# A gated recurrence with both heads of a pair on the partition halves, its scores by quarters of the array, and two pieces of other work moved

## The chip, the cores and the metric

The kernel runs on one core of a Trainium2 chip. The metric is the device time of one execution in microseconds (us), the median of several runs. TensorE (PE in the profile) multiplies matrices, VectorE (DVE), ScalarE (ACT) and GpSimd (POOL) do the rest, SyncE (SP) starts most transfers.

## What is computed

Two blocks follow each other on 1024 tokens of width 1024. The first has two layers; each projects tokens and 256 context tokens, mixes them by three mixers, and sends the result through 16 experts of which each takes its best tokens. The mixer that is changed is a gated linear recurrence with 6 heads of 64 keys and 64 values, run forward and backward and added:

```python
def step(s, xs):                       # one chunk of 64 tokens
    qc, kc, gc, vc = xs
    a = jnp.cumsum(gc, axis=2)
    diff = a[:, :, :, None, :] - a[:, :, None, :, :]
    decay = jnp.exp(jnp.where(causal[:, :, None], diff, -jnp.inf))
    scores = jnp.sum(qc[:, :, :, None, :] * kc[:, :, None, :, :] * decay, axis=-1)
    o = jnp.einsum('bhts,bhsv->bhtv', scores, vc) + jnp.einsum('bhtk,bhkv->bhtv', qc * jnp.exp(a), s)
    a_last = a[:, :, -1:, :]
    s_new = jnp.exp(a_last[:, :, 0, :, None]) * s + jnp.einsum('bhsk,bhsv->bhkv', kc * jnp.exp(a_last - a), vc)
    return s_new, o
```

The layer's modulation (shifts, scales and gates) is a product of the condition with `w_mod`. The second block projects into a gated branch, a delta-rule recurrence (16 heads) and 2048 gate columns, and merges them.

## The kernel before

A product of float32 operands is made of three matmuls on a high and a low part of each (`mm3`, lines 168 to 170): high by high, low by high, and high by low. Weights come from HBM as raw tiles and are split into `whi` (ACT, L151) and `wlo` (VectorE or GpSimd, L154). Such projections run in blocks of 24 matmuls, 8 slices of the contraction by 3, of 512 or 256 columns. After each block `tick` advances the generators in `bg`: that is how the recurrence of one pair of heads is laid among the projection blocks of the next columns. In the recurrence's stages `step` is 2, so each block advances it by two yields. The engines work their own instructions in the order written and wait for one another by semaphores.

`hgrn_pair` runs two generators `hgrn_head` alternately. A head has `hQP` and `hKS` on 128 partitions: the forward direction's 64 keys above, the backward one's below. Chunks of 64 tokens are solved by doubling: at level j (0 to 5) the scores of neighbouring blocks of 2^j tokens are made from queries and keys decayed up to the blocks' border. To have both directions in one matmul of 128 partitions, ACT writes masked queries `hZQ` (L532, L533): a block that is a query block forward is zero in the backward half, and the other way round. L515 multiplies 10 or 8 chunks into one PSUM tile, L522 copies what belongs to the level into `hA` (L520 for the diagonal). Then the level's decays follow: two on `hQP` and one on `hKS` by VectorE, the other on `hKS` by GpSimd (L551), each on 64 partitions, and the product of neighbouring totals `hF` (L558). After the levels the keys are transposed (L577), multiplied with the values (L593), the states are run through in 18 steps (L599), copied into the order of the tokens (`hST`, L601 to L603), and the output is made (L617) and copied out.

The stages in question are six, three pairs in each of two layers: the first two beside a projection of gates (one short and two long blocks in turn), the third beside a token projection in short blocks only.

`prologue` makes the modulation: per round of 2048 columns 8 steps, each of a 1 MB load and four matmuls (L196), then the transposes of the result (L210). Round 0 of layer 1 lies in layer 0's output projection, whose last part is the router and the choice of tokens (`tkv`). Round 1 lies at the end of layer 0's experts (4 steps, into tiles of the expert weights) and at the start of layer 1 (4 steps). In the second block `make_hT` transposes the tokens (L282), and the 2048 gate columns are the last projection beside `rw_scan`.

Of the kernel before, what the change touches and what calls it, by code (L numbers as in the profile page):

```python
# [8 lines left out]
F32 = mybir.dt.float32  # L9
# [10 lines left out]
P = 128  # L20
D = 1024
KT = 8
# [20 lines left out]
class Kern:  # L43
# [273 lines left out]
    def gemm_feat(self, w, c0, n, hi, lo, blocks, evac):  # L317

        for c in range(c0, c0 + n, 256):
            m = min(256, c0 + n - c)  # L320
            us = [self.unit(w[512 * h:512 * (h + 1), c:c + m]) for h in range(2)]
            for f in range(0, m, P):
                for (t0, tn) in blocks(c + f):
# [6 lines left out]
                    self.tick()  # L330


class Mixers(Kern):

    def inproj_setup(self):
# [19 lines left out]
        self.fwd = self.const.tile([P, 2], F32, name="fwd")  # L355
        for h in range(2):
            nc.vector.memset(self.fwd[64 * h:64 * h + 64, h:h + 1], 1.0)
            nc.vector.memset(self.fwd[64 * h:64 * h + 64, 1 - h:2 - h], 0.0)
# [104 lines left out]
    def hgrn_pair(self, l, pr, need, pool):  # L463
        nc = self.nc
        T = NT if need else NLAT
        o = pool.tile([P, NT], F32, name="hgo", tag="hgo", bufs=1)

        heads = [self.hgrn_head(l, 2 * pr + j, T, need, o, pool) for j in range(2)]
        for _ in range(3):
            next(heads[0])  # L470
            yield
        while heads:
            for g in list(heads):
                if next(g, self) is self:
                    heads.remove(g)
                else:
                    yield

        y = pool.tile([P, 10, P], F32, name="hgy", tag="hKT", bufs=1).rearrange("p a b -> p (a b)")
# [14 lines left out]

    def hgrn_head(self, l, h, T, need, oT, pool):
        nc = self.nc
        nch = T // 64
        t = lambda nm, n, b: pool.tile([P, n], F32, name=nm, tag=nm, bufs=b)
        QP, KS, F = t("hQP", NT, 2), t("hKS", NT, 2), t("hF", NT, 2)
        r0 = 64 * (h % 2)  # L500
        for d in range(2):
            nc.sync.dma_start(out=QP[64 * d:64 * d + 64, :T], in_=self.d_q[h // 2][r0:r0 + 64, :T])
        nc.sync.dma_start(out=KS, in_=self.d_k[h])
        nc.sync.dma_start(out=F, in_=self.d_f[h])

        V = pool.tile([P, 10, 64], F32, name="hV", tag="hV", bufs=2)
        nc.sync.dma_start(out=V, in_=self.d_vi[:, 384 + h * 64:384 + (h + 1) * 64].rearrange("(i p) c -> p i c", p=P))
        A = pool.tile([P, 10, 64], F32, name="hA", tag="hA", bufs=2)
        npb = nch // 4

        def scores(zq, seg, j):
            ps = self.pt()
            for c in range(2 * npb):
                cc = seg * 2 * npb + c
                nc.tensor.matmul(ps[64 * (c % 2):64 * (c % 2) + 64, c // 2 * 64:c // 2 * 64 + 64], lhsT=KS[:, cc * 64:(cc + 1) * 64],  # L515
                                 rhs=zq[:, c * 64:(c + 1) * 64], start=True, stop=True)
            src = ps[:, :npb * 64].rearrange("p (n t) -> p n t", t=64)
            dst = A[:, seg * npb:(seg + 1) * npb, :]
            if j < 0:
                nc.scalar.copy(dst, src)  # L520
            else:
                nc.vector.copy_predicated(dst, self.smask[:, j, :].unsqueeze(1).to_broadcast([P, npb, 64]), src)  # L522
# [1575 lines left out]
```

## Time and profile before

| | |
|---|---|
| median of 3 runs | 4155.19 us (4153.61 to 4156.73) |
| the profiled execution | 4153.86 us; its span in the trace 4151.9 us |
| TensorE matmul, weight load | busy 3786.7 us (91%), 3056.1 us (74%) |
| VectorE, ScalarE, GpSimd | 2375.6 (57%), 1750.6 (42%), 1220.0 us (29%) |
| granted TensorE clock | 0.959 of full speed, mean |

Busy times overlap, since the engines work side by side. A matmul of float32 operands that doesn't transpose stands in the trace as two rows, so that counts of score rows are twice those of the code. TensorE's matmul rows overlap each other: their rate is read from start to start, not from the length of a row.

### The profile page before, as it was taken

To read this page: it belongs to the slowest core of one execution; us is meant where nothing else is said; L and a number is where in the kernel's file an instruction comes from. 1 tells how busy PE (TensorE), PEld (TensorE's weight loads), DVE (VectorE), ACT (ScalarE), POOL (GpSimd) and SP (SyncE) were. 2 spreads that over 40 slices of the span, in tenths; PEclk is the share of its full clock that TensorE was granted. 3 is DMA by queue.
4 is the path that set the end of the run, shared out by engine and by line. 5 is a ranking of instruction groups with operands and counts; after the bars stand their busy time and mean duration, and the time that the engine had idled before them with its cause. 6 is when DMAs were issued, how large, how long until landed. Compare 5 with 4: busy or idle time off the path is not lost.

```text
span 4151.9 us, 72321 instructions
## 1 busy us (share of the span) xinstructions
PE 3786.7 (91%) x29022; PEld 3056.1 (74%) x29022; DVE 2375.6 (57%) x3761; ACT 1750.6 (42%) x2935; POOL 1220.0 (29%) x1012
## 2 busy tenths in 40 slices
PE   7998999896999989899889599898989999999998
PEld 5877887764677678778777387676768888887777
DVE  3067745657677632774675799756766353332633
ACT  4145543622555432554362376554564212222522
POOL 2134233422233222432442222104551033211630
PEclk9999999998999999999999799999999999999999
DMA  7733322255799874332223799734544544454732
GB/s 244 233 122 105 86 75 82 71 203 176 271 300 307 277 238 146 117 103 76 80 77 129 255 364 370 234 97 125 152 142 136 153 134 130 143 149 138 248 125 91
DMA packets 543791, 695.78 MB, mean 168 GB/s; under 512 B 162400, under 2 KB 350176, under 8 KB 536800
## 3 DMA queue, kind: packets, MB, share of 16 engines
q1 hardware_dynamic: 531360, 653.40, 48.6%
q0 software_dynamic: 12096, 37.75, 3.7%
q8 instruction: 229, 3.75, 0.4%
q14 instruction: 106, 0.87, 0.1%
HBM read 530.61 MB, written 160.43 MB: 166 GB/s over the span
## 4 chain that ended last, share of the span: by engine, by line
PE 38%; DMA 4%; DVE 4%; POOL 3%; issue 2%; ACT 1%; SPq 0%; DVEq 0%; POOLq 0%; ACTq 0%
PE pg L168 10%; PE pg L170 10%; PE pg L169 10%; POOL Xi L1765 1%; PE pt L1932 1%; POOL Xt L1762 1%; PE pt L1836 1%; DMA raw<-in_w_exp_down_dram 1%; PE pg L667 1%; DVE wlo L154 1%; PE pt L840 1%; PE p L804 1%; DMA no<-ro 1%; ACT whi L151 0%; PE pt L771 0%
## 5 line engine op out<-in xcount | busy, mean ns | idle before, releaser
L154 DVE TENSOR_TENSOR wlo<-raw,whi 128x2048 fp32r<-128x2048 f32 (+2 forms) x320 | 597.1, 1876 | 446.8 <-ACT whi L151 446.2
L168 PE MATMUL pg<-hi,whi 128*128 128x512 f32 (+1 forms) x1808 | 720.6, 399 | 2.0 <-DVE cy L457 1.1
L151 ACT CAST whi<-raw 128x2048 fp32r<-128x2048 f32 (+2 forms) x354 | 531.3, 1503 | 443.5 <-PE pg L169 153.0
L170 PE MATMUL pg<-hi,wlo 128*128 128x512 f32 (+1 forms) x1808 | 699.3, 387 | 0.0
L169 PE MATMUL pg<-lo,whi 128*128 128x512 f32 (+1 forms) x1808 | 698.0, 386 | 0.0
L168 PEld LDWEIGHTS pg<-hi,whi 128*128 128x128 f32 x1808 | 347.1, 192 | 78.4 <-issue 6.1
L169 PEld LDWEIGHTS pg<-lo,whi 128*128 128x128 f32 x1808 | 347.4, 192 | 70.7 <-issue 6.8
L170 PEld LDWEIGHTS pg<-hi,wlo 128*128 128x128 f32 x1808 | 346.7, 192 | 68.2
L169 PE MATMUL pg<-wlo,hi 128*128 128x256 f32 x1200 | 343.5, 286 | 6.4 <-DVE wlo L154 3.8
L168 PE MATMUL pg<-whi,hi 128*128 128x256 f32 x1200 | 345.8, 288 | 1.5 <-ACT whi L151 1.1
L170 PE MATMUL pg<-whi,lo 128*128 128x256 f32 x1200 | 343.0, 286 | 0.0
L169 PEld LDWEIGHTS pg<-wlo,hi 128*128 128x128 f32 x1200 | 230.8, 192 | 16.1 <-issue 7.5
L168 PEld LDWEIGHTS pg<-whi,hi 128*128 128x128 f32 x1200 | 230.4, 192 | 14.6 <-issue 8.6
L170 PEld LDWEIGHTS pg<-whi,lo 128*128 128x128 f32 x1200 | 230.8, 192 | 4.1 <-issue 2.8
L154 POOL TENSOR_TENSOR wlo<-raw,whi 128x1024 fp32r<-128x1024 f32 (+1 forms) x34 | 98.3, 2896 | 409.2 <-ACT whi L151 387.9
L168 PE MATMUL pg<-whi,xh 128*128 128x512 f32 x512 | 209.4, 409 | 0.0
L169 PE MATMUL pg<-wlo,xh 128*128 128x512 f32 x512 | 204.9, 400 | 2.2 <-DVE wlo L154 2.1
L170 PE MATMUL pg<-whi,xl 128*128 128x512 f32 x512 | 204.5, 400 | 0.8 <-DVE xl L1066 0.8
L551 POOL TENSOR_TENSOR hKS<-hKS,hF 64x640 f32<-64x640 f32 x72 | 121.2, 1686 | 181.8 <-PE pt L515 132.8
L1130 POOL DMA_INDIRECT x<-eo,iT x32 | 99.3, 3102 | 244.8 <-DVE eo L1122 232.3
L551 DVE TENSOR_TENSOR hQP<-hQP,hF 64x640 f32<-64x640 f32 (+1 forms) x144 | 146.3, 1016 | 10.2 <-ACT hZQ L532 5.3
L1058 POOL DMA_INDIRECT xg<-xn,iT x32 | 61.1, 1911 | 283.9 <-PE pt L1167 266.9
(457 smaller groups left out, 7988.0 us busy)
## 6 DMA issues: line engine op xcount, KB each, us to landing
raw<-in_w_exp_gate_dram SPq DMA_DIRECT2D x64, 1024.0 KB
raw<-in_w_exp_up_dram SPq DMA_DIRECT2D x64, 1024.0 KB
raw<-in_w_exp_down_dram SPq DMA_DIRECT2D x64, 1024.0 KB
raw<-in_k_win_dram SPq DMA_DIRECT2D x124, 512.0 KB
wm<-in_w_mod_dram SPq DMA_DIRECT2D x36, 1024.0 KB
AR<-AR SPq DMA_DIRECT2D x32, 512.0 KB
BK<-BK SPq DMA_DIRECT2D x32, 512.0 KB
mxr<-mix SPq DMA_DIRECT2D x18, 512.0 KB
```

The lines of the kernel that those rows point to most:

```text
L151: nc.scalar.copy(hi, r)
L154: i = eng.tensor_tensor(out=lo, in0=r, in1=f32(hi), op=ALU.subtract)
L168: mm(out, lhsT=lh, rhs=rh, start=start, stop=False)
L169: mm(out, lhsT=lh, rhs=rl, start=False, stop=False)
L170: mm(out, lhsT=ll, rhs=rh, start=False, stop=stop)
L551: eng.tensor_tensor(out=xv, in0=xv, in1=tv[rows, :m, 1 - o].unsqueeze(2).to_broadcast([64, m, s]), op=ALU.mult)
L667: nc.tensor.matmul(po[64 * j:64 * j + 64, :P], lhsT=u["V"][:, u["blk"][x], j * 64:(j + 1) * 64], rhs=u["pT"][:, x, :], start=x == 0, stop= ...
L804: nc.tensor.matmul(ps[:, c0:c0 + n], lhsT=q[:, j, ql], rhs=KK[:, j, k0:k0 + n], start=first, stop=not first, skip_group_check=True)
L840: nc.tensor.transpose(tp[:, x * P:(x + 1) * P], pr[:, (b0 + x) * P:(b0 + x + 1) * P], self.ident)
L1058: nc.gpsimd.indirect_dma_start(out=g, out_offset=None, in_=d_h[:, :], in_offset=bass.IndirectOffsetOnAxis(ap=iT[:, e:e + 1], axis=0))
L1130: nc.gpsimd.indirect_dma_start(out=d_x[:, :], out_offset=bass.IndirectOffsetOnAxis(ap=iT[:, e:e + 1], axis=0), in_=o, in_offset=None, comp ...
L1762: E.tensor_tensor(out=o, in0=Li[:, j, j + 1:].unsqueeze(2).to_broadcast([P, n, m]), in1=X[:, 0, j, :m].unsqueeze(1).to_broadcast([P, n, m] ...
```

## The change

A pair is one generator. Each direction has its tiles `hKS`, `hQP` and `hF`, with the two heads on the partition halves; the columns of the projection are ordered so that the forward gates of a pair stand before its backward ones. A score matmul takes one head (64 partitions), one direction and one chunk, on a quarter of the array; beyond the diagonal it reads only the 32 query columns that count, and writes them to their places in PSUM, a tile for each head. The masked queries and their tiles are gone. The decays are four on 128 partitions, all on VectorE. Each direction has a state tile of its own, read in any order, so that `hST` is gone; the output comes from two PSUM tiles per head (inter-chunk, by direction) and two per parity of chunk, copied by ACT and added by VectorE. Besides, rounds 0 and 1 of layer 1's modulation are both made in layer 0's output projection; and the first 256 gate columns of the second block are projected while its tokens are transposed.

```diff
+            us = [self.split(r) for r in raws or [self.raw(w[512 * h:512 * (h + 1), c:c + m]) for h in range(2)]]
+            order = [(f, b) for f in range(0, m, P) for b in blocks(c + f)]
+            if before:
+                order.sort(key=lambda o: o[1])
+            for i, (f, (t0, tn)) in enumerate(order):
+                    if before:
+                        before(i)
                     acc = self.pg()
...
     def hgrn_pair(self, l, pr, need, pool):
         nc = self.nc
         T = NT if need else NLAT
...
+        nch = T // 64
+        npb = nch // 4
+        dirs, heads = range(2), range(2)
+        half = lambda x: slice(64 * x, 64 * x + 64)
+        t = lambda nm, n, b, tag=None: pool.tile([P, n], F32, name=nm, tag=tag or nm, bufs=b)
+        K = [t("hKS", NT, HB[0]) for d in dirs]
+        Q = [t("hQP", NT, HB[1]) for d in dirs]
+        F = [t("hF", NT, HB[2]) for d in dirs]
...
+        V = pool.tile([P, 10, P], F32, name="hV", tag="hV", bufs=HB[3])
+        A = [pool.tile([P, 10, 64], F32, name="hA", tag="hA", bufs=2) for h in heads]
+        for d in dirs:
+            nc.sync.dma_start(out=Q[d][:, :T], in_=self.d_q[pr][:, :T])
+            nc.sync.dma_start(out=K[d], in_=self.d_k[2 * pr + d])
+            nc.sync.dma_start(out=F[d], in_=self.d_f[2 * pr + d])
...
+        def scores(seg, j):
+
+            ps = [self.pt() for h in heads]
+            for x in range(npb):
+                for d in dirs:
+                    for par in range(2):
+                        cc = 2 * (seg * npb + x) + par
+                        cs = slice(cc * 64, (cc + 1) * 64)
+                        for h in heads:
+                            out, q = ps[h][half(par), x * 64:x * 64 + 64], Q[d][half(h), cs]
+                            if j >= 0:
+                                out, q = (a.rearrange("p (n b s) -> p n b s", b=2, s=1 << j)[:, :, 1 - d, :] for a in (out, q))
+                            nc.tensor.matmul(out, lhsT=K[d][half(h), cs], rhs=q, start=j >= 0 or x + d == 0, stop=j >= 0 or d == 1,
+                                             skip_group_check=True)
+            return ps
+
+        def keep(ps, seg, j):
+            for h in heads:
+                src = ps[h][:, :npb * 64].rearrange("p (n t) -> p n t", t=64)
+                dst = A[h][:, seg * npb:(seg + 1) * npb, :]
+                if j < 0:
+                    nc.scalar.copy(dst, src)
+                else:
+                    nc.vector.copy_predicated(dst, self.smask[:, j, :].unsqueeze(1).to_broadcast([P, npb, 64]), src)
+
+        for seg in range(2):
+            keep(scores(seg, -1), seg, -1)
...
-        y = pool.tile([P, 10, P], F32, name="hgy", tag="hKT", bufs=1).rearrange("p a b -> p (a b)")
+        for d in dirs:
+            nc.vector.tensor_tensor(out=Q[d][:, :T], in0=Q[d][:, :T], in1=F[d][:, :T], op=ALU.mult)
+        Tot = F
+        for j in range(6):
+            s = 1 << j
+            n = NT // (2 * s)
+            tv = [a[:, :2 * n].rearrange("p (n b) -> p n b", b=2) for a in Tot]
+
+            def decay(X, Tn, d, o):
+                m = Tn // (2 * s)
+                xv = X[d][:, :Tn].rearrange("p (n b s) -> p n b s", b=2, s=s)[:, :, o, :]
+                nc.vector.tensor_tensor(out=xv, in0=xv, in1=tv[d][:, :m, 1 - o].unsqueeze(2).to_broadcast([P, m, s]), op=ALU.mult)
+            ps = scores(0, j)
+            yield
+            ps1 = scores(1, j)
+            keep(ps, 0, j)
+            for d in dirs:
+                if j:
+
+                    pv = Tot[d][:, :4 * n].rearrange("p (n b) -> p n b", b=2)
+                    nc.vector.tensor_tensor(out=Tot[d][:, :2 * n], in0=pv[:, :, 0], in1=pv[:, :, 1], op=ALU.mult)
+                decay(Q, T, d, 1 - d)
+                decay(K, NT, d, d)
+            keep(ps1, 1, j)
+            yield
...
+        for d in dirs:
+
+            KT_ = pool.tile([P, 10, P], F32, name="hKT", tag="hKT", bufs=4)
+            for g in range(0, 10, 4):
...
+            yield
...
+            S = pool.tile([P, 20, 64], F32, name="hSP", tag="hKT", bufs=4)
+            pl, pc = self.p2(), [self.pt() for par in range(2)]
+            at = lambda w: pl[:, w % 2 * 512 + w // 2 * 64:][:, :64] if w < 16 else pc[w % 2][:, (w - 16) // 2 * 64:][:, :64]
+            for i in [8, 9] + list(range(8)):
+                for h in heads:
+                    for par in range(2):
+                        c = 2 * i + par
...
+                            nc.tensor.matmul(at(w)[half(h)], lhsT=KT_[half(par), i, half(h)], rhs=V[half(par), i, half(h)], start=True,
+                                             stop=True, skip_group_check=True)
...
+            for w in range(1, 19):
+                c = place(w)
+                nc.vector.scalar_tensor_tensor(out=S[:, w + 1, :], in0=S[:, w, :], scalar=Tot[d][:, c:c + 1], in1=at(w), op0=ALU.mult,
+                                               op1=ALU.add)
+            SP.append(S)
+            yield
+        for c0, cn in [(0, 16)] + ([(16, 4)] if need else []):
...
+            for kind in range(3):
+                for x in range(cn // 2):
+                    for par in range(2):
+                        i = c0 // 2 + x
+                        c = 2 * i + par
+                        xs = slice(x * 64, x * 64 + 64)
+                        for h in heads:
+                            if kind < 2:
+                                nc.tensor.matmul(ps[h][half(par), xs], lhsT=SP[kind][half(h), 19 - c if kind else (c + 4) % 20, :],
+                                                 rhs=Q[kind][half(h), c * 64:(c + 1) * 64], start=kind + x == 0, stop=kind == 1,
+                                                 skip_group_check=True)
+                            else:
+                                nc.tensor.matmul(pa[par][half(h), xs], lhsT=V[half(par), i, half(h)], rhs=A[h][half(par), i, :], start=True,
+                                                 stop=True, skip_group_check=True)
+            for par in range(2):
+                tk = oT[:, c0 * 64:(c0 + cn) * 64].rearrange("p (n b t) -> p n b t", b=2, t=64)[:, :, par, :]
+                v = lambda a: a[:, :cn * 32].rearrange("p (n t) -> p n t", t=64)
+                for h in heads:
+                    nc.scalar.copy(tk[half(h)], v(ps[h][half(par)]))
+                nc.vector.tensor_tensor(out=tk, in0=tk, in1=v(pa[par]), op=ALU.add)
...
-    def hgrn_head(self, l, h, T, need, oT, pool):
...
-        W = T // 2
-        def masked(j):
-            out = []
-            for seg in range(2):
-
-                ZQ = t("hZQ", NT // 2, 4)[:, :W]
-                v = lambda a, o: a.rearrange("p (n b s) -> p n b s", b=2, s=1 << j)[:, :, o, :]
-                q = QP[:, seg * W:(seg + 1) * W]
-                nc.scalar.activation(v(ZQ, 1), v(q, 1), AF.Copy, scale=self.fwd[:, 0:1])
-                nc.scalar.activation(v(ZQ, 0), v(q, 0), AF.Copy, scale=self.fwd[:, 1:2])
-                out.append(ZQ)
-            return out
...
-            decay(QP, T, up, 1, nc.vector)
-            decay(QP, T, dn, 0, nc.vector)
-            if j < 5:
-                ZQ = masked(j + 1)
-            decay(KS, NT, up, 0, nc.vector)
-            decay(KS, NT, dn, 1, nc.gpsimd)
...
-        nc.scalar.copy(ST[0:64], SP[0:64])
-        nc.scalar.copy(ST[64:128, 4:20], SP[64:128, 19:3:-1])
-        nc.scalar.copy(ST[64:128, 0:4], SP[64:128, 3::-1])
...
-                    if i + j >= 4:
+                    if i + j >= 2:
                         next(self.held, None)
...
-            if l:
-                for _ in range({2: 2, 5: KT - AHEAD - 2, 8: 1}.get(i, 0)):
-                    next(self.held, None)
...
-                    self.held = self.prologue(1, [0])
+                    self.held = self.prologue(1, [0, 1])
...
+            if need:
+                self.acc_ctx.close()
+                self.acc_psum = None
...
-            if need:
-                self.wm_tile = lambda: self.wset[0].tile([P, 2048], F32, name="raw", tag="raw", bufs=6)
-                self.held = self.prologue(1, [1])
-                for _ in range(AHEAD):
-                    next(self.held)
...
-                    for _ in self.make_hT(xs, 8, lambda: (None, self.npre), hi, lo, hb, lambda i: None):
-                        pass
+                    first = []
+                    hT = self.make_hT(xs, 8, lambda: (None, self.npre), hi, lo, hb,
+                                      lambda i: first.extend(self.raws_tok(w, 7296)) if i == 0 else None)
+                    next(hT)
+
+                    def before(i):
+                        for _ in range((1, 2, 2, 0)[i]):
+                            next(hT, None)
+                    self.gemm_feat(w, 7296, 256, hi, lo, blocks, gates(hb), first, before)
...
-                    self.gemm_feat(w, 7296, 2048, hi, lo, blocks, ev)
+                    self.gemm_feat(w, 7296 + 256, 2048 - 256, hi, lo, blocks, gates(gp))
                     self.drain()
```

VectorE, first pair of layer 0, its first level (rows from the one that applies F to the queries). Names are those of the code: `hQP` queries, `hKS` keys, `hF` totals, `hA` kept scores, `pt` the PSUM tile of the scores. Before:

```order
L539 TENSOR_TENSOR hQP<-hQP,hF 128x1280
L551 TENSOR_TENSOR hQP<-hQP,hF 64x640
L522 COPY_PREDICATED hA<-smask,pt 128x320
L551 TENSOR_TENSOR hQP<-hQP,hF 64x640
L522 COPY_PREDICATED hA<-smask,pt 128x320
L551 TENSOR_TENSOR hKS<-hKS,hF 64x640
L558 TENSOR_TENSOR hF<-hF 128x640
```

Now:

```order
L520 TENSOR_TENSOR hQP<-hQP,hF 128x1280 x2
L514 COPY_PREDICATED hA<-smask,pt 128x320 x2
L530 TENSOR_TENSOR hQP<-hQP,hF 128x640
L530 TENSOR_TENSOR hKS<-hKS,hF 128x640
L530 TENSOR_TENSOR hQP<-hQP,hF 128x640
L530 TENSOR_TENSOR hKS<-hKS,hF 128x640
L514 COPY_PREDICATED hA<-smask,pt 128x320 x2
L539 TENSOR_TENSOR hF<-hF 128x640 x2
```

The 64-partition decays of one head, with the fourth on GpSimd, have become four of 128 partitions for both heads, and copies and totals of both heads stand together.

TensorE, the same pair, between its first scores (`hQP`) and the second level; the L168 to L170 rows around are projection blocks. Before, a block is cut by scores (a piece of it):

```order
L170 MATMUL pg<-hi,wlo 128x512
L515 MATMUL pt<-hZQ,hKS 64x64 x10
L168 MATMUL pg<-hi,whi 128x512
L515 MATMUL pt<-hZQ,hKS 64x64 x10
L169 MATMUL pg<-lo,whi 128x512
```

Now (the end of one block, the scores of a level, the start of the next block):

```order
L168 MATMUL pg<-hi,whi 128x512
L169 MATMUL pg<-lo,whi 128x512
L170 MATMUL pg<-hi,wlo 128x512
L503 MATMUL pt<-hQP,hKS 64x64 x80
L168 MATMUL pg<-hi,whi 128x512
```

All scores of a level and of both heads stand in one run between two whole blocks, seven times in a pair.

TensorE, the end of layer 0's output projection: `acc` is the modulation's product, `oz`, `ohf`, `ols` and `oaf` are the router's steps for the last tokens, `modr` the modulation's result, `tkv` the choice of tokens. Before:

```order
L196 MATMUL acc<-wor,silu_c 32x512 x8
L947 MATMUL pt<-k_ident,oaf_8929 32x128
L924 MATMUL pt<-k_ident,oz 128x128 x8
L930 MATMUL pt<-ohf,wr 32x128 x8
L935 MATMUL pt<-k_sel_397,ols 128x16
L947 MATMUL pt<-k_ident,oaf_8930 32x128
L210 MATMUL pt<-k_ident,modr 128x128 x4
L1005 MATMUL pt<-k_ident,tkv 128x48
```

Now:

```order
L210 MATMUL pt<-k_ident,modr 128x128 x4
L923 MATMUL pt<-k_ident,oz 128x128 x8
L929 MATMUL pt<-ohf,wr 32x128 x4
L196 MATMUL acc<-wor,silu_c 32x512 x4
L929 MATMUL pt<-ohf,wr 32x128 x4
L196 MATMUL acc<-wor,silu_c 32x512
L934 MATMUL pt<-k_sel_392,ols 128x16
L196 MATMUL acc<-wor,silu_c 32x512 x4
L946 MATMUL pt<-k_ident,oaf_9573 32x128
L196 MATMUL acc<-wor,silu_c 32x512 x15
L210 MATMUL pt<-k_ident,modr 128x128 x4
L1004 MATMUL pt<-k_ident,tkv 128x48
```

Six steps of the second round stand between the router's last rows and behind them, ahead of the choice of tokens.

## Rows read from the trace of the kernel before

**Rows 1.** The page, its first line: the span of the execution.

```profile
span 4151.9 us, 72321 instructions
```

**Rows 2.** Busy time by stretch: stretch and length, busy us (count), clock, DMA.

```profile
227.85:330.20 102.35, 93.88 (x1189) 78.51 (x1188) 70.47 (x123) 51.45 (x94) 34.02 (x25) 0.97 0.37 110
...
sum 654.65, PE 595.94 PEld 516.11 DVE 438.06 ACT 317.96 POOL 207.64; mean PE 99.32 PEld 86.02 DVE 73.01 ACT 52.99 POOL 34.61
```

**Rows 3.** Timeline of TensorE: start, us, work, count [idle before, releaser].

```profile
227.41 0.28 PE L168 MATMUL pg<-hi,whi 128*128 128x256 f32 x1
227.53 0.28 PE L169 MATMUL pg<-lo,whi 128*128 128x256 f32 x1
...
227.85 1.39 PE L515 MATMUL pt<-hQP,hKS 128*64 128x64 f32 x40
229.17 0.50 PE L168 MATMUL pg<-hi,whi 128*128 128x512 f32 x1
...
229.73 0.39 PE L170 MATMUL pg<-hi,wlo 128*128 128x512 f32 x1
...
231.80 0.39 PE L170 MATMUL pg<-hi,wlo 128*128 128x512 f32 x1
```

**Rows 4.** Timeline of TensorE, first and following row of the state matmuls.

```profile
284.41 0.50 PE L593 MATMUL p<-hV,hKT 64*64 64x64 f32 x17
...
285.74 0.50 PE L168 MATMUL pg<-hi,whi 128*128 128x512 f32 x1
```

**Rows 5.** Busy time by stretch, the same matmuls (their count behind PEld).

```profile
284.40:285.60 1.20, 1.20 (x80) 1.19 (x76) 1.17 (x2) 0.39 (x1) 1.03 (x1) 1.00 1.12 416
```

**Rows 6.** Timeline of TensorE, second block, parts of 32x32.

```profile
2897.60 0.69 PE L1791 MATMUL pt<-X,Lo 32*32 32x32 f32 x32
2898.22 0.51 PE L168 MATMUL pg<-hi,whi 128*128 128x512 f32 x1
```

**Rows 7.** Instructions of lines 515 and 617: idle before them until (us, times).

```profile
  POOL hKS L551: 29.2, 19
...
  DVE hKS L551: 20.5, 13
...
  ACT hST L602: 23.8, 13
```

**Rows 8.** Timeline of TensorE, a block of 24 behind a wait.

```profile
276.56 0.69 PE L577 MATMUL pt<-k_ident,hKS 128*128 128x128 f32 x2 [2.84 <-DVE hA L522]
276.90 0.56 PE L168 MATMUL pg<-hi,whi 128*128 128x256 f32 x1
...
281.95 0.41 PE L170 MATMUL pg<-hi,wlo 128*128 128x256 f32 x1
```

**Rows 9.** Timeline of VectorE, first pair of layer 0.

```profile
233.12 0.51 DVE L522 COPY_PREDICATED hA<-smask,pt 128x320 f32<-128x320 int32 x1
233.67 0.82 DVE L551 TENSOR_TENSOR hQP<-hQP,hF 64x640 f32<-64x640 f32 x1
...
234.94 1.98 DVE L551 TENSOR_TENSOR hKS<-hKS,hF 64x640 f32<-64x640 f32 x1
237.02 0.83 DVE L558 TENSOR_TENSOR hF<-hF 128x640 f32<-128x640 f32 x1
```

**Rows 10.** Timeline of GpSimd at the same time.

```profile
234.24 2.00 POOL L551 TENSOR_TENSOR hKS<-hKS,hF 64x640 f32<-64x640 f32 x1 [0.69 <-POOL stg L413]
```

**Rows 11.** Timeline of TensorE, end of layer 0's output projection.

```profile
986.58 1.92 PE L196 MATMUL acc<-wor,silu_c 128*32 128x512 f32 x16
...
1014.32 0.31 PE L1005 MATMUL pt<-k_ident,tkv 48*128 48x48 f32 x1 [12.75 <-DVE tkv L980]
```

**Rows 12.** Timeline of TensorE, end of the second block's recurrence.

```profile
3820.65 0.60 PE L1891 MATMUL pt<-R,XT 128*64 128x64 f32 x4 [0.57 <-ACT R L1881]
3821.62 1.15 PE L1891 MATMUL pt<-R,XT 128*64 128x64 f32 x28 [0.37 <-DVE R L1881]
...
3829.13 2.08 PE L168 MATMUL pg<-yh,whi 128*128 128x512 f32 x4 [3.33 <-ACT yh L1424]
```

More of the change, by code (lines that the diff above doesn't have):

```diff
@@ L315, in gemm_tok, with gemm_feat @@
             self.tick()
[L317 removed]
+    def gemm_feat(self, w, c0, n, hi, lo, blocks, evac, raws=None, before=None):
         for c in range(c0, c0 + n, 256):
             m = min(256, c0 + n - c)
[L321 to L323 removed]
+            us = [self.split(r) for r in raws or [self.raw(w[512 * h:512 * (h + 1), c:c + m]) for h in range(2)]]
[5 more added lines that the diff above has]
+                        before(i)
                     acc = self.pg()
@@ new lines, in hgrn_pair @@
+        for d in dirs:
+            pv = Tot[d][:, :40].rearrange("p (n b) -> p n b", b=2)
+            nc.vector.tensor_tensor(out=Tot[d][:, 40:60], in0=pv[:, :, 0], in1=pv[:, :, 1], op=ALU.mult)
+        Tot = [a[:, 40:60] for a in Tot]
+        SP = []
+        for d in dirs:
+            KT_ = pool.tile([P, 10, P], F32, name="hKT", tag="hKT", bufs=4)
+            for g in range(0, 10, 4):
+                m = min(4, 10 - g)
+                tp = self.pt()
+                for i in range(m):
+                    nc.tensor.transpose(tp[:, i * P:(i + 1) * P], K[d][:, (g + i) * P:(g + i + 1) * P], self.ident)
+                nc.scalar.copy(KT_[:, g:g + m, :].rearrange("p a b -> p (a b)"), tp[:, :m * P])
+            yield
+            S = pool.tile([P, 20, 64], F32, name="hSP", tag="hKT", bufs=4)
[5 more added lines that the diff above has]
+                        c = 2 * i + par
+                        w = 19 - c if d else (c + 4) % 20
+                        if w < 19:
+                            nc.tensor.matmul(at(w)[half(h)], lhsT=KT_[half(par), i, half(h)], rhs=V[half(par), i, half(h)], start=True,
+                                             stop=True, skip_group_check=True)
+            place = lambda w: 19 - w if d else (w - 4) % 20
+            nc.vector.memset(S[:, 0, :], 0.0)
+            nc.vector.tensor_copy(S[:, 1, :], at(0))
+            for w in range(1, 19):
[3 more added lines that the diff above has]
+            SP.append(S)
+            yield
@@ new lines, in hgrn_pair @@
+        oT = o = t("hgo", NT, 4, "hKT")
+        for c0, cn in [(0, 16)] + ([(16, 4)] if need else []):
+            ps, pa = [[self.pt() for x in range(2)] for y in range(2)]
+            for kind in range(3):
[18 more added lines that the diff above has]
+                nc.vector.tensor_tensor(out=tk, in0=tk, in1=v(pa[par]), op=ALU.add)
+            yield
@@ L1373, in block2, with gates, ev @@
         self.step = 1
+        def gates(pool):
+            def ev(c, t0, tn, acc):
+                f = (c - 7296) // P
+                s = pool.tile([P, 512], F32, name="sgt", tag="gu", bufs=3)
+                self.act(s, acc, AF.Tanh, scale=0.5)
+                d = d_ga if f < 8 else d_gb
+                self.nc.sync.dma_start(out=d[f % 8 * P:(f % 8 + 1) * P, t0:t0 + tn], in_=s)
+            return ev
         wst, mst = ExitStack(), ExitStack()
```

129 lines of the change are left out of this document (7 added, 122 removed).

## The prediction

> **What bounds the kernel now.** The page first: one execution spans 4151.9 us [rows 1]; it was timed at 4153.86, 1.3 under the median of 4155.19, and I make the sum against it. Next the busy time by stretch, over the six stages (three pairs of heads, two layers) in which projection and recurrence share TensorE. They take 654.65 us; TensorE is busy 595.94 of them and the next engine, VectorE, 438.06 [rows 2]. So TensorE sets the pace, but it stands still for 58.7 us there, and some of what counts as busy is slow.
>
> The timeline of TensorE gives the rates. A projection matmul of 256 columns follows the last after 0.12 us, one of 512 after (231.80 - 229.73)/9 = 0.23 [rows 3]. With 24 in a block these are 2.8 and 5.5 us. A pair of layer 0 has four times one short and two long blocks, 55.2 us; the third pair has 720 short rows, 84 us. Layer 1, counted the same way, has 49.6, 49.6 and 78.6. Sum 372 us, which the change leaves alone. Forty score rows take 229.17 - 227.85 = 1.32 us, 33 ns each [rows 3]; a pair's 560 score rows, its output, state and transpose rows come to some 32 us in layer 0 and 27 in layer 1, in all 177. 654.65 - 372 - 177 leaves **about 105 us of waits and slow clock**. The views of the two lines name the waits: before scores, GpSimd's decay of hKS 29.2 us and VectorE's 20.5, before the output rows the copies to hST 23.8 (loads and matmuls together) [rows 7]. After a wait of 2.84 us the next block of 24 short rows ran from 276.90 to 281.95, 0.21 us a row where 0.12 is usual [rows 8, 3]: the lower of TensorE's two clocks, at 2.1 us per block. I count nine such stretches in the stages.
>
> **The change, part by part.** *Scores.* Before, a head's 20 chunks are multiplied over 128 partitions (both directions, masked queries as zeros); now each 64x64 quarter of the array does one head, one direction, with half the columns. A level of a pair has 160 rows where two heads had 80. The nearest rows are the quarters that make the states: 76 loads between 284.41 and 285.74, 17.5 ns each with the change of form at the end, about 15.5 inside a run [rows 4, 5]. These move 64 columns, the new ones 32. Bounds: the time does not fall with the columns (15.5, 17.4 us a pair plus run ends of 1, against 18.5 before: no change), or it halves (-8 us a pair). For halving nothing speaks: 32 matmuls of 32 columns on 32x32 parts took 0.62 us, 19 ns each [rows 6]. I take 15.5. That the columns are now strided, by up to every second, no row of the trace shows for a matmul; above, I allow a burst of twice the time, +15 us a pair in layer 0.
>
> The Trainium skill, "TensorEngine Tiling (Array Packing)", Instruction Overhead, says that a matmul costs about as much with one moving column as with 60, and that no tiling factor should be taken from a dimension that is already small. The rows of 32 columns agree [rows 6]. By it, dropping masked columns gives nothing; by the halving, 48 us over six pairs.
>
> *Output, states.* 160 output rows a pair at 33 ns become 240 at about 16.5, -1.3 us; scores come in 7 runs a pair instead of some 16 pieces of 20 to 80 rows, and the output rows no longer change form for every kind and head; for the ends of runs saved I put -2, an estimate. That is -3.3 a pair, -20 in all.
>
> *Decays.* Before, each head and level has three on VectorE and one on GpSimd, of 64 partitions. On VectorE one took 0.82 us with GpSimd idle, 1.98 beside GpSimd's own, which took 2.00 [rows 9, 10]. Now a level of the pair has four of 128 partitions, all on VectorE. Their price isn't in the trace. Nearest is the product of totals, 128 partitions by 640, 0.83 us [rows 9]; above stands 1.98. I take 0.82, since nothing of the decays is left on GpSimd: 3.3 us a level, 3.5 with the signal, in which TensorE has a 5.5 or 2.8 us block. GpSimd's gate rows still meet some of them.
>
> Behind long blocks the decays are hidden. Behind short ones (two a pair) TensorE waits 0.7. For the third pair every block between levels is short, and VectorE itself is the limit: between two levels' decays come four masked copies of 0.51 and two products of up to 0.83 [rows 9], 3.7 us, so the period is 3.3 + 3.7 = 7.0 at its longest and 5.8 at its shortest against 5.1 of TensorE work: 6.5 us a pair. Before, the other head's scores and decays lay in these gaps. 18 us for the ends of the six stages (state chains, first loads), 13 + 6 for the levels, and 12 for low clock after what stays long make 49.
>
> Gone also are ACT's maskings and its copies to hST with the waits for them (23.8 above). ACT wasn't the limit, so nothing else comes from it. The loads on SP's queue have the same bytes, in one place per pair; Q and K of the next pair wait for buffers of this one, and two projection blocks lie between load and first score.
>
> Stages: 105 - 49 = **-56**, with -20: **-76 us**.
>
> *Modulation.* Eight more load-and-multiply steps of layer 1's second round go to the end of layer 0's output projection: two of those steps, 16 rows, take 1.92 us [rows 11], so eight take some 7.7. Six are queued among the last router rows there, in front of and behind the row that feeds the top-k, after which TensorE waits 12.75 us anyway [rows 11]. Behind lies cover; in front, two to three steps and their 1 MB loads can hold the top-k up. Four leave the end of layer 0's experts, where TensorE waits a little later, and four layer 1's start, where it is busy: 3.8 us and the transposes behind them. Bounds -8 and +6; I take -4. Cover gone, it would be the +6.
>
> *Gates.* The first 256 gate columns, four blocks of 5.5 us, move from beside the scan of the second block to its start, between the transposes. The work is the same. At the end, the scan's last chunk but one loses its cover. Its last chunk shows waits of 0.57 and 0.37 and then 3.33 for yh [rows 12]; one more set of those, with a state update between: +3, bounds 0 and +6. At the start, transposes were dense, so I count no gain.
>
> Sum: -76 - 4 + 3 = -77 against 4153.86, and with the 1.3 to the median about **4078**.
>
> **Rivals.**
> 1. *Waits stay.* One chain per pair instead of two heads that fill each other's gaps: everything after the last score (transposes, two state chains in turn, output) is exposed. For it: the old waits on hST and hA were at just those places. Against: the pair's tail has blocks between its steps. If all 105 us stay, only the -20 and -1 are left: about 4134.
> 2. *Slower decays on one chain, and the kernel gets slower.* If a decay of 128 partitions takes 1.67 to 1.98 as the contended ones did, a level's four take 6.7 or more. A long block then lets 1.4 us show and a short one 4.1; with 4 long and 2 short in a pair 14 us, and 25 in the third pair, about 53 in layer 0 and 45 in layer 1: 98 where I count 19, and 10 for the clock, +89. That gives 4167. It decides from 1.6 us a decay on. Against: GpSimd has no decays any more, and 0.82 is seen whenever it is idle [rows 9].
> 3. *Strided columns at twice the time.* 960 rows a pair with +15.5 ns, 15 us in layer 0 and 12 in layer 1, about +80: 4158, no change.
> 4. *Columns set the rate.* The scores fall by 8 us a pair, 48 in all, but VectorE's 5.8 to 7.0 a level stands in the way: about half arrives, 4052.
>
> **How the numbers follow.** The forecast, its own range 4055 to 4105: 0.55. Rival 1: 0.17. Rival 4 or fewer waits than I leave (none at all would be 4029): 0.14. Rival 3: 0.06; rival 2: 0.08. The range for 8 in 10 runs from 4035 to 4138; it leaves out rivals 2 and 3 and the outer part of rival 4. A change of 0.2%, 8.3 us, is about what a measurement of this kernel tells from none. Faster: 0.55 + 0.17 + 0.14 = 0.86, and a little of rival 3, 0.87. Same: most of rival 3 and of the edge of rival 2, 0.06. Slower: 0.07.
>
> **What would show it.** Right: the six stages near 90, 90, 123, 80, 80 and 113 us; score runs of 160 rows in 2.3 to 2.7 us; decays of 0.82 us by the median; waits before scores only behind short blocks and in the third pair; GpSimd no longer among the releasers of scores. Wrong: runs of 160 rows well over 3 us (rival 3) or near 1.2 (rival 4); decays over 1.2 us (rival 2); TensorE idle in the tail of each pair, released by the state chain or the copies of the transposed keys (rival 1). For the modulation: the first matmul of layer 0's experts should not come later after the end of the output projection than it does now.

## The result

The changed kernel took 4075.76 us in the median (4073.24 to 4081.1, 4 runs) against 4154.4 us (4153.0 to 4156.73, 4 runs) of the kernel before: a ratio of 0.9814, 95% interval 0.9802 to 0.9827. It is 1.9% faster; the forecast of 4078 was 2 us off. The page of one execution (4077.6 us) begins, and has as its chain:

```profile
span 4075.8 us, 78529 instructions
PE 3747.1 (92%) x32478; PEld 3031.5 (74%) x32478; DVE 2252.8 (55%) x3680; ACT 1586.7 (39%) x2610; POOL 1086.8 (27%) x939
...
PE 33%; DMA 5%; DVE 3%; POOL 3%; issue 3%; ACT 1%; SPq 0%; DVEq 0%; POOLq 0%; ACTq 0%
```

Busy time by stretch, for the whole of layer 0's and of layer 1's projections with recurrence (from the first gate block to the first block of what follows; columns as in [rows 2], which begin 58 and 52 us later). Before:

```profile
169.80:572.20 402.40, 372.59 (x4280) 325.75 (x4279) 234.21 (x383) 180.84 (x326) 119.26 (x85) 0.97 0.36 109
1587.10:1950.05 362.95, 334.05 (x3650) 285.69 (x3650) 217.61 (x377) 162.25 (x301) 110.34 (x83) 0.98 0.38 112
```

and the changed kernel:

```profile
168.70:542.50 373.80, 358.70 (x6201) 317.56 (x6200) 171.97 (x347) 94.66 (x162) 51.94 (x49) 0.99 0.38 118
1554.70:1879.10 324.40, 316.04 (x5187) 278.03 (x5186) 154.21 (x335) 86.41 (x140) 51.90 (x47) 0.99 0.40 126
```

67 of the 76 us between the two spans are here: 28.6 in layer 0, 38.5 in layer 1. TensorE's idle time, length less busy, fell from 29.8 + 28.9 to 15.1 + 8.4 us, and its granted clock rose. VectorE is busy 126 us less, although all decays are now its own; ACT lost 162.

Where the recurrence sits, the timelines show what was forecast. VectorE's decays of one level (the second, first pair of layer 0):

```profile
250.32 0.81 DVE L530 TENSOR_TENSOR hQP<-hQP,hF 128x640 f32<-128x640 f32 x1
251.05 0.81 DVE L530 TENSOR_TENSOR hKS<-hKS,hF 128x640 f32<-128x640 f32 x1
251.78 0.81 DVE L530 TENSOR_TENSOR hQP<-hQP,hF 128x640 f32<-128x640 f32 x1
252.52 0.82 DVE L530 TENSOR_TENSOR hKS<-hKS,hF 128x640 f32<-128x640 f32 x1
```

TensorE's next scores, 160 rows between two whole blocks, 257.97 - 255.50 = 2.47 us or 15.4 ns a row:

```profile
255.50 2.54 PE L503 MATMUL pt<-hQP,hKS 64*64 64x32 f32 x160
257.97 0.50 PE L168 MATMUL pg<-hi,whi 128*128 128x512 f32 x1
```

What the scores still wait for, by the view of their line (to set beside [rows 7]):

```profile
L503 PE MATMUL pt<-hQP,hKS x6048: 186/219/312, 232.5 to 1807.1; 64*64 64x32 f32 x168, 64*64 64x64 f32 x28
...
  issue: 22.2, 33
  DVE hQP L520: 4.5, 4
  DVE hKS L530: 3.4, 4
```

GpSimd is no longer among the releasers of scores. "issue" is time for which the trace shows no releaser; before, it was 22.2 us as well.

### The profile page after: what moved, and what is told of

The parts are those of the page before. It is cut to its first block, busy times and chain, and to the rows that moved or that the text cites. A ratio compares the mean times of both kernels' runs of the same rounds, so it can differ in the third digit from the quotient of the medians.

```text
span 4075.8 us, 78529 instructions
## 1 busy us (share of the span) xinstructions
PE 3747.1 (92%) x32478; PEld 3031.5 (74%) x32478; DVE 2252.8 (55%) x3680; ACT 1586.7 (39%) x2610; POOL 1086.8 (27%) x939
## 5 line engine op out<-in xcount | busy, mean ns | idle before, releaser
L168 PE MATMUL pg<-hi,whi 128*128 128x512 f32 (+1 forms) x1808 | 717.6, 397 | 3.1 <-DVE cy L462 1.1
L170 PE MATMUL pg<-hi,wlo 128*128 128x512 f32 (+1 forms) x1808 | 695.8, 385 | 0.0
L168 PEld LDWEIGHTS pg<-hi,whi 128*128 128x128 f32 x1808 | 345.1, 191 | 79.1 <-issue 6.5
L170 PEld LDWEIGHTS pg<-hi,wlo 128*128 128x128 f32 x1808 | 344.7, 191 | 67.3 <-issue 0.2
L168 PE MATMUL pg<-whi,hi 128*128 128x256 f32 x1200 | 345.8, 288 | 2.0 <-ACT whi L151 1.1
L170 PE MATMUL pg<-whi,lo 128*128 128x256 f32 x1200 | 342.6, 285 | 0.8 <-POOL lo L298 0.7
L168 PEld LDWEIGHTS pg<-whi,hi 128*128 128x128 f32 x1200 | 230.8, 192 | 13.4 <-issue 8.4
L169 PEld LDWEIGHTS pg<-wlo,hi 128*128 128x128 f32 x1200 | 230.9, 192 | 11.1 <-issue 6.1
L170 PEld LDWEIGHTS pg<-whi,lo 128*128 128x128 f32 x1200 | 231.0, 192 | 7.2 <-issue 5.2
L168 PE MATMUL pg<-whi,xh 128*128 128x512 f32 x512 | 209.3, 409 | 0.0
L170 PE MATMUL pg<-whi,xl 128*128 128x512 f32 x512 | 204.6, 400 | 0.8 <-DVE xl L1065 0.8
L391 ACT COPY stg<-pg 128x256 f32<-128x256 f32 x118 | 44.0, 373 | 296.2 <-PE pg L170 263.1
L169 PE MATMUL pg<-wlo,mxh 128*128 128x512 f32 x288 | 119.4, 415 | 8.3 <-DVE wlo L154 5.4
```

The source lines that it names most:

```text
L168: mm(out, lhsT=lh, rhs=rh, start=start, stop=False)
L169: mm(out, lhsT=lh, rhs=rl, start=False, stop=False)
L170: mm(out, lhsT=ll, rhs=rh, start=False, stop=stop)
L391: nc.scalar.copy(s, acc)
```

## The experiments

Times of whole runs scatter here by some 10 us, stretches of the trace by one or two, so the table compares stretches of TensorE's timeline (us from marker to marker; each row is one execution, named after the runs told below): **stages**, the two stretches above; **proj**, layer 0's output projection; **choice**, from its last block to the first expert's; **start**, end of layer 0's experts to layer 1's gates; **scan**, from the last expert block through the second block's scan; **branch**, the product of the scan's branch behind it.

```
                    stages L0  stages L1   proj  choice  start    scan  branch
before                 402.5     362.9    167.1    41.8  146.0  1175.8   210.4
changed                373.7     324.4    169.7    49.7  134.9  1176.0   204.2
recurrence alone       377.3     326.4    163.5    41.7  154.2  1172.0   212.6
modulation alone       402.4     361.7    170.4    48.2  136.5  1170.7   208.6
gates alone            402.6     363.2    168.0    42.1  149.2  1174.4   203.1
all columns            372.1     325.9    167.7    48.3  134.2  1177.2   205.2
decay on GpSimd        391.3     333.7    169.5    49.5  137.1  1177.9   206.0
before, all VectorE    384.8     339.5    164.9    44.0  145.6  1173.0   209.3
steps earlier          373.5     324.7    179.1    41.9  135.4  1175.3   206.2
no key decay           371.2     322.8    170.6    49.0  135.3  1176.6   206.9
output apart           371.2     324.2    170.2    50.1  133.8  1175.0   204.3
changed again          373.2     325.0    166.0    48.4  134.8  1178.4   206.6
```

**Each part alone.** Three kernels: the one before with only the new `hgrn_pair` (and the order of columns it needs), with only the modulation's lines, with only the gates' lines of the change, as in the diff above.

> The recurrence's part alone, modulation and gates as before. My sum had -76 us for it. By the markers in the two traces the six stages gave 28.6 us in layer 0 and 38.5 in layer 1, so I now expect -67 against the kernel before, some 4087. A rival: the stages are only where the gain shows, and part of it comes from the other two parts (earlier loads, another PSUM split); then this run stays at 4100 or above.

> The modulation's part alone. The prediction had -4 us. Between the traces the end of the output projection and the choice of tokens got 10.5 us longer and the experts' end with layer 1's start 13.1 shorter: I expect -3, between -5 and 0. A rival: the six steps behind the router hold the top-k back by their loads, and layer 1's start gains nothing when the recurrence is the old one: slower by 5 or more.

> The gates' part alone. The prediction had +3 us, from the waits of one more uncovered chunk. Between the traces the stretch from the end of the experts to the end of the scan got 0.2 us longer, and what follows 5 us shorter, where less of TensorE ran at the lower clock: I expect -5 to 0. A rival: what follows is shorter by chance or by the recurrence, and the uncovered chunk shows: +1 to +4.

Recurrence alone: 4085.71 us against 4150.74 of the kernel before on that chip, ratio 0.9845 (0.9832 to 0.9858), some 64 us, and 62 in the stages. The gain is the recurrence's own; the rival falls. Modulation alone: 0.9994 (0.9985 to 1.0004); gates alone: 0.9998 (0.9988 to 1.0009). Neither can be told from no change by its whole time. By the table the modulation's proj, choice, experts (1.8 shorter, not in the table) and start come to -1.6, in the changed kernel to -2.6. These are differences from one execution, and start scatters by 8.6 us among the four rows without the move; by means (seven rows with the steps moved as in the change, four without) proj and choice got 3.3 + 6.6 us longer, start and experts 13.5 + 2.3 shorter: -5.9. For the gates all twelve rows speak: with them moved (eight rows) the scan's stretch is 1174.4 to 1178.4 us, mean 1176.4, without (four rows) 1170.7 to 1175.8, mean 1172.9; the branch behind it 203.1 to 206.9, mean 205.3, against 208.6 to 212.6, mean 210.2.

**Do columns count?** In the changed kernel:

```diff
-                            if j >= 0:
-                                out, q = (a.rearrange(...)[:, :, 1 - d, :] for a in (out, q))
```

> The changed kernel with all 64 query columns in every score matmul, as for the diagonal, also the masked ones; the second direction then overwrites the first, so the off-diagonal scores of the forward direction are lost. Theory, that a row on a quarter costs 15.4 ns whatever it moves: runs of 160 rows stay at 2.5 us and the time within 3 us of the changed kernel. Rival, that moving columns count: runs of 160 near 3.5 to 5 us and 70 to 200 us more.

Ratio 0.9839 (0.9824 to 0.9855), the stages 1.6 us shorter and 1.5 longer than in the changed kernel. The timeline of TensorE, the same level as above:

```profile
255.51 2.58 PE L501 MATMUL pt<-hQP,hKS 64*64 64x64 f32 x160
258.03 0.50 PE L168 MATMUL pg<-hi,whi 128*128 128x512 f32 x1
```

2.52 us with 64 columns, 2.47 with 32. Leaving out the masked columns gives nothing; its use is that one tile can serve both directions without a masked copy. That strided columns at twice the time hide a gain from half of them is ruled out by the changed kernel's own levels: in the second pair, level 0 reads every second column and level 5 reads 32 side by side, and both runs take 2.46 to 2.47 us:

```profile
336.07 2.54 PE L503 MATMUL pt<-hQP,hKS 64*64 64x32 f32 x160
338.53 0.39 PE L168 MATMUL pg<-hi,whi 128*128 128x256 f32 x1
...
373.84 2.54 PE L503 MATMUL pt<-hQP,hKS 64*64 64x32 f32 x160
376.31 0.50 PE L168 MATMUL pg<-hi,whi 128*128 128x512 f32 x1
```

**GpSimd beside VectorE, from both sides.** The changed kernel with one decay moved to GpSimd:

```diff
-                nc.vector.tensor_tensor(out=xv, ...)
+                (nc.gpsimd if X is K and d else nc.vector).tensor_tensor(out=xv, ...)
```

> The changed kernel with one of the four decays of each level, the backward keys', on GpSimd again. If the two engines slow each other as in the kernel before, the three left on VectorE take 1.2 to 2.0 us by the median instead of 0.82 and GpSimd's some 2 us or more, since it now has 128 partitions; TensorE then waits before most score runs and the six stages get 20 to 60 us longer together. Rival: VectorE has a quarter less to do and the stages stay within 5 us or get shorter.

and the kernel before with its one decay taken from GpSimd:

```diff
-            decay(KS, NT, dn, 1, nc.gpsimd)
+            decay(KS, NT, dn, 1, nc.vector)
```

> The kernel before with its fourth decay on VectorE too, and nothing else changed. If it was the meeting of GpSimd and VectorE that made the old waits, the decays on VectorE fall to 0.82 us by the median, the waits of some 50 us on the two engines' key decays mostly go, and the time falls by 15 to 35. Rival, that 64 partitions a decay are the cost: VectorE has eight of 0.82 a level and pair, 6.6 us, is the limit, and the time stays within 8 us or rises.

The first: 4105.06 us, ratio 0.9886 (0.9870 to 0.9901); the stages 17.6 + 9.3 = 27 us longer than in the changed kernel. The view of the decays' line (min, median, max in ns):

```profile
L530 DVE TENSOR_TENSOR hQP<-hQP,hF x72: 677/810/1976, 247.4 to 1837.0; 128x640 f32<-128x640 f32 x36, 128x512 f32<-128x512 f32 x36
...
L530 POOL TENSOR_TENSOR hKS<-hKS,hF x36: 1314/1820/2365, 247.6 to 1834.8; 128x640 f32<-128x640 f32 x36
L530 DVE TENSOR_TENSOR hKS<-hKS,hF x36: 810/1930/2489, 248.2 to 1835.2; 128x640 f32<-128x640 f32 x36
```

VectorE's decay of the keys, which begins while GpSimd's runs, takes 1930 ns in place of 818; the queries' keep 810. I had expected all three to be slow; one was enough. The timelines of both engines show that it is not a slowing of whatever overlaps:

```profile
247.43 0.83 DVE L530 TENSOR_TENSOR hQP<-hQP,hF 128x640 f32<-128x640 f32 x1 [1.87 <-PE pt L503]
247.59 2.37 POOL L530 TENSOR_TENSOR hKS<-hKS,hF 128x640 f32<-128x640 f32 x1 [2.21 <-PE pt L503]
248.17 2.47 DVE L530 TENSOR_TENSOR hKS<-hKS,hF 128x640 f32<-128x640 f32 x1
```

The queries' decay overlaps the start of GpSimd's by 0.67 us and still takes 0.83; the keys' decay begins behind that start and ends 0.68 us behind GpSimd's end, about its own length alone. All 32 decays of VectorE that begin during one of GpSimd's end 0.54 to 0.69 us behind it, and so do all 62 in the kernel before. The rows read as if the engine that comes second waits for the first to end.

The second is the surprise: one word changed in the kernel before, 4118.41 us, ratio 0.9922 (0.9907 to 0.9937), some 32 us, and the stages 17.7 + 23.4 = **41 us** shorter; the other stretches of this execution were together 5 us longer, without a cause in the edit. Its decays and its scores' waits:

```profile
L551 DVE TENSOR_TENSOR hKS<-hKS,hF x144: 798/822/2897, 237.9 to 1884.3; 64x640 f32<-64x640 f32 x144
...
its engine sat idle before it (us, times) until:
  ACT hZQ L533: 26.5, 44
  DVE hKS L551: 17.1, 19
  ACT hZQ L532: 11.0, 14
```

VectorE's key decays had a median of 877 ns before, a mean of 1272 in layer 0 and up to 2371. The wait on GpSimd's decay, 29.2 us [rows 7], is gone; what holds the scores now is ACT's masking, which waits for VectorE's decays of the queries (91.4 us, 44 times). The stages by busy time, columns as above:

```profile
172.50:557.30 384.80, 362.80 (x4281) 317.44 (x4280) 238.40 (x419) 180.62 (x325) 52.78 (x49) 1.00 0.38 114
1572.50:1912.00 339.50, 325.33 (x3650) 280.32 (x3649) 215.48 (x413) 161.91 (x301) 49.58 (x47) 0.99 0.40 118
```

TensorE's idle time is 36 us in place of 59, and it runs at the lower clock for 3 us in place of 41, which at half speed is worth 19: together the 41. From this kernel to the changed one the stages lose another 11.1 + 15.1 = 26 us. The masking's wait goes with the new layout, but it is the smaller part: idle time falls by 13 us more, while the lower clock, 17 us in the changed kernel, takes 7 back; the rest, some 20, is TensorE's work itself.

**What is left in the stages.** The changed kernel without the line `decay(K, NT, d, d)`:

> The changed kernel without the decays of the keys, half of the four; keys keep their undecayed values, so scores, states and output are not those of the reference. It shows what VectorE still costs the stages. If what waits are left before scores come from the decays, they go and the stages get 8 to 15 us shorter together; rival: the waits left come from the diagonal's copies, the first product with the totals and the output's copies, and the stages change by under 5.

The stages got 2.5 + 1.6 = 4.1 us shorter (whole time 4090.79 us, ratio 0.9862, 0.9847 to 0.9877, no gain). The rival holds: with half the decays gone the waits before scores on the first product (L520) are still 6.0 us. TensorE's idle time in the stages didn't fall at all (26.5 us against 23.5); what fell is the time at the lower clock, from 17 us to none, worth 8.5. So the decays of the keys are hidden; those of the queries were not taken out, and for them it isn't shown.

The second, and last, thing tried there is the output's wait. After the first part of the output and ahead of the second, two yields in place of one:

```diff
             yield
+            for _ in range(self.step - 1 if need and not c0 else 0):
+                yield
```

> The changed kernel with the output's second part (the four context chunks of layer 0) one projection block later in the first two pairs, so that it doesn't wait for the copies of the first part out of PSUM. In the changed kernel TensorE waits 1.08 us there, and in each of layer 0's pairs a stretch of 3.4 us at the lower clock begins 2.7 us after that wait. If the wait brings the stretch, both go in the first two pairs and layer 0's stages get 4 to 6 us shorter; the third pair, whose order doesn't change, keeps both. Rival, that the narrow matmuls of the output bring the clock down by themselves: the stretch stays or moves, and the stages get 0 to 2 us shorter.

> The changed kernel itself, beside the run above on the same chip, as the measure for it: a ratio to the kernel before of 0.981 to 0.985, layer 0's stages 373 to 374 us.

The wait of 1.08 us left the first two pairs, and layer 0's stages took 371.2 us where the changed kernel took 373.2 beside it (373.7 in its first execution): -2.0, the rival's size. It isn't the wait's: other waits grew, so that TensorE's idle time there fell by only 0.4 us (14.7 to 14.3), and the rest is 3.4 us less at the lower clock, worth 1.7. The whole time doesn't show it: ratio 0.9825 (0.9802 to 0.9849) against 0.9821 (0.9807 to 0.9835). And my theory of the stretch at the lower clock falls by the changed kernel itself. Its first execution:

```profile
310.30:313.60 3.30, 3.30 (x29) 2.60 (x22) 0.57 (x2) 2.51 (x6) 0.00 (x0) 0.50 0.78 238
```

and its second, the same place in the program, with 1.08 us of waiting ahead of it in both (the figure behind POOL, 0.50 and 1.00, is the clock):

```profile
311.10:314.50 3.40, 3.40 (x24) 2.77 (x19) 0.57 (x2) 2.99 (x6) 0.00 (x0) 1.00 0.82 242
```

The same wait was followed by the lower clock once and not the other time; what decides it, these runs don't tell.

**The modulation's steps.** From the third tile on two steps per tile, so that none is left behind the last block:

```diff
-                    if i + j >= 2:
-                        next(self.held, None)
+                    for _ in range(2 if i + j >= 3 else 1):
+                        next(self.held, None)
```

> The changed kernel with two steps of the modulation per tile from the third tile of the output projection on, so that no step is left among the router's last rows. If those steps and their loads hold the choice of tokens up, the time from the last projection matmul of layer 0 to the first of its experts goes back from 49.5 us to the 41.7 of before or less; the output projection itself gets some 6 us longer, since the steps stand in it, and the sum is -2 to -8 with the earlier end. Rival: the loads of 2 MB a tile hold up the output projection, and the sum is 0 or worse.

4081.7 us, ratio 0.9831 (0.9818 to 0.9844). The sum that I expected did not come, the rival's did: choice falls from 49.7 to 41.9 us, as before the change, but proj rises by 9.4, so that the two are 1.6 us longer together. TensorE in the changed kernel, ahead of the choice (`tkv`):

```profile
978.43 1.17 PE L196 MATMUL acc<-wor,silu_c 128*32 128x512 f32 x8 [2.64 <-DMA wor<-in_w_mod_dram]
980.95 1.93 PE L196 MATMUL acc<-wor,silu_c 128*32 128x512 f32 x8 [1.35 <-DMA wor<-in_w_mod_dram]
984.63 1.93 PE L196 MATMUL acc<-wor,silu_c 128*32 128x512 f32 x8 [1.75 <-DMA wor<-in_w_mod_dram]
989.71 1.11 PE L210 MATMUL pt<-k_ident,modr 128*128 128x128 f32 x4 [3.15 <-DVE modr L206]
990.76 0.34 PE L1004 MATMUL pt<-k_ident,tkv 48*128 48x48 f32 x1
```

and with the steps earlier:

```profile
986.06 0.60 PE L946 MATMUL pt<-k_ident,oaf 128*32 128x128 f32 x2 [4.14 <-DVE oaf L943]
998.08 0.34 PE L1004 MATMUL pt<-k_ident,tkv 48*128 48x48 f32 x1 [11.42 <-DVE tkv L979]
```

In the changed kernel the last steps wait for their loads, the transposes for VectorE, and `tkv` follows them without a wait of its own: the choice is held up behind work that isn't its own. Taken away there, the same matmuls cost as much in the projection. It isn't the loads, as the rival had it: TensorE's idle time in proj is 13.3 us against 13.7, so the steps filled none of it, and 64 more rows of 0.12 us with 6 us more at the lower clock make up the 9.4 and a little more. No version tried beats the changed kernel by more than the runs scatter.

## Why the prediction was right, and where not

The time came out 2 us from the forecast, but as a sum whose parts were off by up to 9 us and made up for each other; that it hit so closely is luck. Measured, the parts are -67, -3 to -6 and about -1.5, some -71 to -74; the whole time gave -79 at first and -74 when the changed kernel ran again.

**Stages, -76 forecast, -67 by the markers, -64 by the run of the part alone.** TensorE's own work, -20: summed from start to start over every score, output, state and transpose matmul it fell from 177 to 156 us, -21. The rates held: 15.4 ns a score row where 15.5 was taken, 0.82 us a decay (818 ns by the median) where 0.82 was taken, the waits behind short blocks 0.91 and 0.70 us where 0.7 was reckoned.

Waits and slow clock, -56 (105 to 49): this term was mis-sized. Idle time fell by 35 (58.7 to 23.5), and time at the lower clock from some 41 us (ten stretches, where I counted nine) to 17, which at half speed is worth 12: together -47. (Of the -21 above, 6 are slow rows and stand in the 12 too; without them it is -15, and the projection blocks lost another 5.)

The step that failed is the first, "leaves about 105 us of waits and slow clock", a remainder: 58.7 of idle and half of 41 make 79. With the slow rows counted at full speed, the projection blocks took 396 us where I had put 372, nearly all of the excess in rows at either end of a run of blocks, and the recurrence's own matmuls with the norm's 181 where I had put 177: that is about the rest. A remainder holds every error of the terms before it. What stays, put at 49, was too high as well: 23.5 of idle and half of 17 make 32.

The prediction also didn't ask how much of the waits a single cause held. It named GpSimd's 29.2 and VectorE's 20.5 us [rows 7] and saw 0.82 against 1.98 [rows 9], and still counted the gain as one of layout. Of the stages' 67 us, 41 come with one decay moved from GpSimd to VectorE.

**Rivals.** Rival 2, decays of 1.67 to 1.98 us on one chain, had the right mechanism: put back for one of four decays it cost 27 us. It didn't happen, since nothing on GpSimd met the decays for long. Rival 1: waits in the tail are at most 0.64 us a pair for the state chain and, in layer 0 alone, 1.24 for the copies; two more in layer 1, 0.88 and 1.76 us, have no releaser in the trace. Rivals 3 and 4: strided columns cost no more, and half the columns no less. (Half of rival 4's 48 us taken from 4078 is 4054, not 4052.) The rule of the Trainium skill, "TensorEngine Tiling (Array Packing)", Instruction Overhead, by which one moving column costs as much as 60, said the same of the number of columns; the runs of 2.47 us with 32 columns and 2.52 with 64, just beyond its 60, bear it out for these two widths.

**Modulation, -4 forecast, -2.6 in these two traces, -5.9 by the means of the table.** Right in kind, and the size can't be told closer than that: choice and proj lost 10.5 us, experts and start got 13.1 back. The cover named, TensorE's 12.75 us of waiting for `tkv` [rows 11], was no cover to the end: the loads and VectorE's share of the steps pushed the last of them past it.

**Gates, +3 forecast, about -1.5.** The scan's stretch got 3.5 us longer by the means of the table, the forecast's number, but not by its mechanism, the waits of one more uncovered chunk. That chunk shows waits:

```profile
3751.76 0.59 PE L1892 MATMUL pt<-R,XT 128*64 128x64 f32 x4 [1.29 <-ACT R L1882]
3753.19 1.15 PE L1892 MATMUL pt<-R,XT 128*64 128x64 f32 x28 [0.83 <-DVE R L1882]
...
3758.51 0.50 PE L168 MATMUL pg<-yh,whi 128*128 128x512 f32 x1
```

The wait of 3.33 us for `yh` [rows 12] is gone: the first operands of the next product are there when the two chunks are through. From the last gate block to that product, before and now:

```profile
3818.60:3829.10 10.50, 6.12 (x130) 4.84 (x128) 2.85 (x5) 5.87 (x10) 0.99 (x1) 0.99 0.78 244
...
3739.00:3758.50 19.50, 17.01 (x330) 14.43 (x328) 13.74 (x25) 9.68 (x18) 2.95 (x2) 0.91 0.62 200
```

Idle time fell there, from 4.4 us to 2.5; what rose is the time at the lower clock, by the means of the table's rows from 0.2 us to 6.7, worth some 3. The +3 came true by another term than the one reckoned. What follows I had left out of the sum: the branch's product, 4.9 us shorter. Its busy time, before:

```profile
3829.10:4039.60 210.50, 199.52 (x830) 158.66 (x831) 102.03 (x105) 78.37 (x111) 99.34 (x66) 0.97 0.57 186
```

and now:

```profile
3758.50:3962.70 204.20, 194.53 (x833) 155.63 (x830) 97.94 (x102) 76.92 (x110) 100.99 (x66) 0.99 0.57 187
```

Idle time is less (11.0 us to 9.7), and the clock higher, which is the larger part of the 6.3 us here. That the gates' move does it is shown by the two groups in the table; how, by an earlier start of the weights' split or otherwise, was not tried.

## What to carry to other kernels

Before a layout is changed, look whether two engines hold each other up: one line of the timeline with and one without the neighbour (0.82 and 1.98 us here) is enough, and moving one instruction may give half of what a rewrite gives (here 41 of 67 us in the stages, 32 of 64 in the whole time). Between 32 and 64 columns, small matmuls on array quarters cost by the row and not by the column, so pack heads and directions, and don't hope for columns left out. Put a price on each wait by its own row, not by a remainder; read idle time and granted clock apart, since here a stretch got shorter by the clock alone more than once; and count a moved step's loads and its other engines' instructions where they will queue.

## What was unexpected of the hardware

A GpSimd product of two tensors took 1820 ns for 128 partitions where it took 1753 for 64 in the kernel before (medians). VectorE's decay that began beside it took 1930 ns in place of 818, and ended 0.54 to 0.69 us behind it every time, 32 of 32, as in the kernel before, 62 of 62; the decay that had begun ahead of it kept 0.82 us by the median of that run (31 of them, at most 1.23). A score row on a quarter took 15.4 ns with 32 and 15.7 with 64 columns. And stretches at the lower clock came at other places in two executions of one kernel (310 us in one, full speed there in the other), behind the same wait.
